# Hybrid attention layer: the probabilities-times-values matmuls of the two head groups made ready together and issued as a pair

## The chip, the cores and the metric

The kernel runs on one core of one Trainium2 chip. The metric is device microseconds from the first to the last instruction of one execution; times of the kernel are medians of several runs. One execution was also taken by the hardware profiler, and all rows below are from it.

## What is computed

One decoder layer for 512 tokens of width 1024 in float32: a norm, an input projection, two attention parts side by side, one output projection, a second norm and a squared-ReLU MLP. The attention is what matters here. Both parts have eight heads of 64 columns. The first part ("NSA") has two groups of four heads with keys and values of their own, and three branches, each with a softmax: over compressed blocks, over selected blocks and over a window. The second part ("DSA") has one set of keys and values for its eight heads, and keeps the 256 best keys of each query. The core of every branch is the same:

```python
s = jnp.einsum('bqhd,bqkd->bhqk', qb, kg) * scale
p = masked_softmax(s, mask)
return jnp.einsum('bhqk,bqkd->bqhd', p.astype(vg.dtype), vg)
```

The change touches the last line alone, the product of probabilities with values.

## The kernel before, in words

**Work units.** Attention runs in 12 units, one for each branch (s: selected, w: window, d: DSA) and each tile of 128 queries (j = 0 to 3); `UNITS` (line 51) gives their order. A unit has two halves. `heads_steps` (line 855) makes, for each of eight heads, scores with two matmuls (lines 872 and 873) into a PSUM bank of tag S, one VectorE pass that adds the mask and finds the maximum (875), and one exponential on ScalarE (876), which leaves the probabilities in SBUF with queries on the partitions. `out_steps` (line 879) first scales the probabilities (`scale`, lines 885 to 893; three heads of four on VectorE, one on GpSimd), then goes over the key blocks kb = 0 to j of 128 keys. For each block and each group g of four heads, `tr` (line 895) transposes four 128 x 128 pieces on TensorE (898) into a PSUM bank of tag T, of which there are two, and copies the bank to an SBUF tile `pt` of 128 x 512 (ScalarE, line 903; VectorE, line 901, for group 1 where j is 3). `pv` (line 906) then multiplies: for each group one matmul (908) with 64 columns of values as weights and the 128 x 512 tile `pt` as the moving operand. Group 0 writes partitions 0 to 63 of the PSUM bank `O`, group 1 partitions 64 to 127. The compressed branch (`cmp_steps`, line 918) does the same with 31 keys, once for each tile of queries: transposes at 953, copies at 955, two matmuls at 960. In all there are 3 x (1 + 2 + 3 + 4) + 4 = 34 such pairs of matmuls, 68 matmuls.

**Dependences.** Each matmul of line 908 or 960 needs the copy of its own group. The matmul of group 0 does not wait for the copy of group 1.

**Order of the work.** The program traces, slot by slot, the heads of one unit interleaved with the output half of the unit before (lines 1071 to 1096), and with other groups of steps, which the table `PLAN` (line 41) puts at slots: sums of the modulation vectors (`vec_steps`, line 703, matmuls at 717; their column sums at 756), the output projection (`outp_steps`, line 998, matmuls at 1008), the loads and splits of its weights (117), the residual and the second norm (1032 to 1058). In program order the transposes of block kb + 1 come before `pv(kb)`. The order in which each engine finally gets its instructions is not this one: the framework's scheduler makes it (line 1198, `schedule_with_timeline_sim=True`), from what is ready in a timeline of its own. Each engine then runs its instructions in that fixed order and waits by semaphores.

**Around it.** The projections come before (up to about 190 us of the span), the MLP after (`up`, line 1115, and `down`, line 1156, from about 397 us to the end).

A float32 matmul stands in the trace as two matmul records with a weight load each; the rows of lines 908 and 960 therefore count two for each matmul.

Of the kernel before, what the change touches and what calls it, by code (L numbers as in the profile page):

```python
# [17 lines left out]
P = 128  # L18
# [19 lines left out]

# Groups of steps in program order: the slot where each begins, and the slots it spreads over.
# Slots 0 to 18 are the projections' pipeline, slots from 19 on the units of attention.  # L40
PLAN = dict(
# [13 lines left out]
def mix(*lists):  # L55
    """One list of the steps of several, each list spread evenly."""
    items = []
    for li, steps in enumerate(lists):
        for i, f in enumerate(steps):
            items.append(((i + 0.5) / len(steps), li, i, f))  # L60
    return [it[3] for it in sorted(items, key=lambda z: z[:3])]
# [8 lines left out]
def layer_kernel(  # L70
# [41 lines left out]
    def bank(tag, name, dt=F32):  # L112
        return psp.tile([P, 512], dt, tag=tag, name=name, bufs=4 if tag == "S" else 2)

    def split(hi, lo, src, eng=V):
        A.copy(hi, src)  # L116
        eng.tensor_tensor(lo, src, hi.bitcast(F32), op=OP.subtract)  # L117
# [3 lines left out]

    # ------------------------------------------------------------ first loads
    wa = w_ada[0].rearrange("(p k) n -> p k n", k=KT)
# [43 lines left out]

    # ------------------------------------------------------------ constants
    ident = cst.tile([P, P], F32, name="ident")
# [23 lines left out]
    def rstd_of(dst, ss):  # L193
        """1 / sqrt(D) of the reciprocal root mean square, from the sums of squares of two halves."""
        m = st([P, 1], "ms")
        G.tensor_scalar(m, ss[:, 0:1], ss[:, 1:2], D * EPS, op0=OP.add, op1=OP.add)  # L196
        G.tensor_tensor(dst, m, mhalf, op=OP.pow)

    # ------------------------------------------------ columns, rope tables
    colT = cst.tile([P, P], F32, name="colT")  # L200
# [40 lines left out]

    # -------------------------------------------------------------- x norms
    rstd = cst.tile([P, NT], F32, name="rstd")
# [17 lines left out]

    # ------------------------- first norm's shift and scale, chunks A and B
    hh = ht("hh", "hh_1")
# [5 lines left out]
    def mod_acc(k):  # L269
        """Sums over the eight slices of c * w_ada, the two halves on different engines."""  # L270
        acc = m2(f"macc_{k}").rearrange("p (u v n) -> p u v n", u=2, v=2)
        macc[k] = acc
        sl = [mod_w[k][i // 4][:, :, i % 4, :] for i in range(KT)]
        steps = []
        for i in range(4):
            dst = acc[:, 1] if i == 0 else sl[i]
            steps.append(lambda i=i, dst=dst: A.activation(dst, sl[i], AF.Copy, scale=c_sb[:, i:i + 1]))
            if i > 0:
                steps.append(lambda i=i: G.tensor_tensor(acc[:, 1], acc[:, 1], sl[i], op=OP.add))
        steps.append(lambda: V.tensor_scalar(acc[:, 0], sl[4], c_sb[:, 4:5], None, op0=OP.mult))  # L280
        for i in range(5, KT):
            steps.append(lambda i=i: V.scalar_tensor_tensor(acc[:, 0], sl[i], c_sb[:, i:i + 1], acc[:, 0],  # L282
                                                            op0=OP.mult, op1=OP.add))
        steps.append(lambda: V.tensor_tensor(acc[:, 0], acc[:, 0], acc[:, 1], op=OP.add))
        return steps
# [95 lines left out]

    # ----------------------------------------------------- projection stages
    def w_unit(view, nm, n=512, eng=V):
# [13 lines left out]
    def rope(src, t, nh, nm, eng):  # L397
        """src: [P, nh, 64] view, rotated in place."""
        t1 = m2("ra_" + nm)[:, :nh * 64].rearrange("p (h d) -> p h d", d=64)
# [143 lines left out]

    # --------------------------------------------------------------- indexer
    work = [None] + [cst.tile([P, (t + 1) * P], F32, name=f"wk_{t}") for t in range(1, NT)]
# [28 lines left out]

    # -------------------------------------------------------------- compress
    kcx = cst.tile([P, 2, 2, 32], F32R, name="kcx")
# [76 lines left out]

    # ------------------------------------------------- G vectors and columns
    res = {}
# [47 lines left out]
    def vec_steps(c0, nm, finish):  # L703
        """finish(half, ps) gets 32 times the sums over 32 partitions each, which add up to c @ w_ada."""
        stt = {}
# [55 lines left out]

    # ------------------------------------------------ the projection pipeline
    def w_in_chunk(c0, c1, nm, eng=V):
# [80 lines left out]

    # ------------------------------------------------------------- attention
    On, Od, o_hl = {}, {}, {}

    class Unit:
        """Eight heads of one branch for one tile of queries."""

# [28 lines left out]
        def out_steps(self, O, first, last):  # L879
# [15 lines left out]
            def tr(kb, g):  # L895
                tp = bank("T", f"tp_{nm}{j}{kb}{g}")
                for i in range(4):
                    PE.transpose(tp[:, i * P:(i + 1) * P], self.P[g * 4 + i][:, kb * P:(kb + 1) * P], ident)  # L898
                pt = m2(f"pt_{nm}{j}{kb}{g}")
                if g == 1 and j >= 3:  # L900
                    V.tensor_copy(pt, tp)
                else:
                    A.copy(pt, tp)
                pts[kb, g] = pt

            def pv(kb):
                for g in range(2):
                    PE.matmul(O[j][g * 64:(g + 1) * 64, :], vn[kb][:, self.vsl[g]:self.vsl[g] + 64], pts[kb, g],  # L908
                              start=(first and kb == 0), stop=(last and kb == j))
            steps += [lambda: scale(0), lambda: scale(1)]  # L910
# [7 lines left out]
    def cmp_steps(j):  # L918
# [31 lines left out]
        def tr(g):  # L950
            tp = bank("T", f"tpc_{j}{g}")
            for i in range(4):
                PE.transpose(tp[0:32, i * P:(i + 1) * P], stt["p"][:, g * 4 + i, :], ident)
            pt = m2(f"ptc_{j}{g}")
            A.copy(pt[0:32, :], tp[0:32, :])
            stt[g] = pt

        def pv():
            for g in range(2):
                PE.matmul(On[j][g * 64:(g + 1) * 64, :], vc[0:31, g, :], stt[g][0:31, :], start=False, stop=True)  # L960
        return [scores, soft1, soft2], [lambda: tr(0), lambda: tr(1), pv]
# [16 lines left out]

    # ---------------------------------------------------- output projection
    wov = w_out[0].rearrange("(b g i d) n -> b g d i n", b=2, g=2, d=64)  # L980
# [81 lines left out]

    # --------------------------------------------- attention, woven together
    wa1, wb1 = wout_steps("a", 1), wout_steps("b", 1)
# [30 lines left out]

    # ------------------------------------------------------------------ MLP
    wuv = w_up[0].rearrange("(k p) n -> p k n", p=P)
# [104 lines left out]
```

## Time and profile before

| what | us |
|---|---|
| median of 3 runs | 760.26 |
| lowest and highest run | 757.55, 763.36 |
| span of the profiled execution | 759.8 |
| TensorE busy in it | 717.0 |
| VectorE busy | 482.5 |
| ScalarE busy | 343.0 |
| GpSimd busy | 160.4 |

The profiled execution has one time on its page, its span from the first to the last instruction; nothing beside it is counted. It is 0.4 us under the median of the runs. Busy times are sums over the whole span; a share of them says nothing of a single stage, so the rows below are taken by stretch.

### The profile page before, as it was taken

Reading aid. Unit: us, or ns where it says so; the run is one execution under the profiler, and the core shown is the slowest. Engines: PE = TensorE matmul, PEld = TensorE weight load, DVE = VectorE, ACT = ScalarE, POOL = GpSimd, SP = SyncE. Lnnn points to the kernel's source line nnn. Section 1 sums busy time; section 2 is a strip of 40 time slices with the busy share of each in tenths; the row PEclk is TensorE's granted clock in tenths of the full one; section 3 lists DMA queues with packets and bytes.
Section 4 is the critical chain, followed back from the end, with each engine's and each line's share of the span. In section 5 each row is a group of like instructions: output and inputs, shape, how many; then the busy total and the mean of one; then the engine's idle time right before and its main releaser. Section 6 shows DMA issues by size and latency. Waiting matters only on the chain.

```text
span 759.8 us, 9830 instructions
## 1 busy us (share of the span) xinstructions
PE 717.0 (94%) x3473; PEld 545.5 (72%) x3473; DVE 482.5 (64%) x1014; ACT 343.0 (45%) x715; POOL 160.4 (21%) x223
## 2 busy tenths in 40 slices
PE   3878989899999999999999999999999999999995
PEld 2667976687755565545579888888888888788884
DVE  5996636979998777772566547463645535344547
ACT  6643683624786568663255532323133223313312
POOL 4663093553632143310202000000000000000003
PEclk9897998878999999999899999999999999999998
DMA  8975452430005380460331336231524332241202
GB/s 277 345 240 160 139 157 66 122 101 1 2 20 153 108 219 1 112 220 2 112 100 40 110 111 194 91 131 60 190 83 141 109 111 82 61 163 56 83 1 110
DMA packets 67610, 87.13 MB, mean 115 GB/s; under 512 B 3973, under 2 KB 38889, under 8 KB 67562
## 3 DMA queue, kind: packets, MB, share of 16 engines
q1 hardware_dynamic: 67562, 86.52, 36.6%
q8 instruction: 27, 0.44, 0.2%
q14 instruction: 21, 0.17, 0.1%
HBM read 84.40 MB, written 2.10 MB: 114 GB/s over the span
## 4 chain that ended last, share of the span: by engine, by line
PE 78%; DVE 10%; DMA 5%; ACT 2%; issue 2%; SPq 2%; POOL 1%; POOLq 0%; DVEq 0%; ACTq 0%
PE up L1115 22%; PE dn L1156 21%; PE O L908 6%; PE op L1008 6%; PE pj_C L316 3%; DMA wv_g<-in_w_ada_dram 2%; PE pj_D L316 2%; PE pA L316 1%; PE tp_d L898 1%; PE tp_w L898 1%; PE tp_s L898 1%; DMA x<-in_x_dram 1%; DVE macc L282 1%; DVE wk L569 1%; DVE m L566 1%
## 5 line engine op out<-in xcount | busy, mean ns | idle before, releaser
L1115 PE MATMUL up<-hh,uh_U 128*128 128x512 f32 (+1 forms) x288 | 104.6, 366 | 0.7 <-ACT hh L116 0.7
L1115 PE MATMUL up<-hh,ul_U 128*128 128x512 f32 (+1 forms) x288 | 105.0, 366 | 0.0
L1115 PE MATMUL up<-hl,uh_U 128*128 128x512 f32 (+1 forms) x288 | 103.9, 366 | 0.4 <-DVE hl L117 0.4
L1156 PE MATMUL dn<-uh_D,al 128*128 128x512 f32 x256 | 99.6, 389 | 0.0
L1156 PE MATMUL dn<-uh_D,ah 128*128 128x512 f32 x256 | 98.7, 391 | 0.0
L1156 PE MATMUL dn<-ul_D,ah 128*128 128x512 f32 x256 | 98.5, 389 | 0.0
L196 POOL TENSOR_SCALAR ms<-sy 128x1 f32<-128x1 f32 x4 | 3.6, 908 | 341.7 <-ACT fj L1135 341.7
L117 DVE TENSOR_TENSOR ul_D<-rw_D,uh_D 128x1024 fp32r<-128x1024 f32 (+1 forms) x35 | 41.3, 1181 | 47.5 <-ACT uh_D L116 45.4
L1162 DVE TENSOR_TENSOR y<-dn,y 128x512 f32<-128x512 f32 x56 | 38.2, 689 | 49.1 <-PE dn L1156 49.1
L1115 PEld LDWEIGHTS up<-hh,uh_U 128*128 128x128 f32 x288 | 54.3, 189 | 9.7 <-ACT hh L116 0.9
L1119 ACT ACTIVATE rl<-up 128x512 f32<-128x512 f32 x32 | 19.1, 596 | 92.7 <-PE dn L1156 59.2
L1115 PEld LDWEIGHTS up<-hh,ul_U 128*128 128x128 f32 x288 | 54.3, 189 | 8.7
L1115 PEld LDWEIGHTS up<-hl,uh_U 128*128 128x128 f32 x288 | 53.7, 189 | 9.4 <-DVE hl L117 0.6
L116 ACT CAST uh_U<-rw_U 128x1024 fp32r<-128x1024 f32 x32 | 33.7, 1052 | 57.3 <-PE dn L1156 51.9
L116 ACT CAST uh_D<-rw_D 128x1024 fp32r<-128x1024 f32 (+1 forms) x36 | 36.3, 1010 | 49.5 <-PE up L1115 37.5
L1156 PEld LDWEIGHTS dn<-uh_D,ah 128*128 128x128 f32 x256 | 48.0, 188 | 10.2 <-issue 0.2
L1156 PEld LDWEIGHTS dn<-uh_D,al 128*128 128x128 f32 x256 | 48.0, 188 | 10.1 <-issue 0.2
L1156 PEld LDWEIGHTS dn<-ul_D,ah 128*128 128x128 f32 x256 | 48.1, 188 | 10.0
L117 DVE TENSOR_TENSOR ul_U<-rw_U,uh_U 128x1024 fp32r<-128x1024 f32 x32 | 39.1, 1221 | 12.9 <-ACT uh_U L116 12.0
L1120 DVE TENSOR_TENSOR rl<-rl 128x512 f32<-128x512 f32 x32 | 22.1, 690 | 34.8 <-ACT rl L1119 34.8
L116 ACT CAST ah<-rl 128x512 fp32r<-128x512 f32 x32 | 19.9, 621 | 29.3 <-DVE rl L1120 29.3
L117 DVE TENSOR_TENSOR al<-rl,ah 128x512 fp32r<-128x512 f32 x32 | 22.0, 688 | 11.0 <-ACT ah L116 11.0
(409 smaller groups left out, 1591.8 us busy)
## 6 DMA issues: line engine op xcount, KB each, us to landing
rw_U<-in_w_up_dram SPq DMA_DIRECT2D x32, 512.0 KB, 4.5
rw_D<-in_w_down_dram SPq DMA_DIRECT2D x32, 512.0 KB, 3.7
wm<-in_w_ada_dram SPq DMA_DIRECT2D x32, 256.0 KB, 5.1
wv_g<-in_w_ada_dram SPq DMA_DIRECT2D x8, 512.0 KB, 6.9
rwo_a<-in_w_out_dram SPq DMA_DIRECT2D x16, 256.0 KB, 5.1
wv_a<-in_w_ada_dram SPq DMA_DIRECT2D x8, 512.0 KB, 4.0
rwo_b<-in_w_out_dram SPq DMA_DIRECT2D x16, 256.0 KB, 4.2
wv_sh<-in_w_ada_dram SPq DMA_DIRECT2D x8, 512.0 KB, 3.6
```

What stands on the lines that cost most here:

```text
L116: A.copy(hi, src)
L117: eng.tensor_tensor(lo, src, hi.bitcast(F32), op=OP.subtract)
L282: steps.append(lambda i=i: V.scalar_tensor_tensor(acc[:, 0], sl[i], c_sb[:, i:i + 1], acc[:, 0], op0=OP.mult, op1=OP.add))
L316: PE.matmul(ps[:, :n], l[:, t, k, :], r[:, k % 2, :n], start=(k == 0 and i == 0), stop=(k == KT - 1 and i == 2))
L898: PE.transpose(tp[:, i * P:(i + 1) * P], self.P[g * 4 + i][:, kb * P:(kb + 1) * P], ident)
L908: PE.matmul(O[j][g * 64:(g + 1) * 64, :], vn[kb][:, self.vsl[g]:self.vsl[g] + 64], pts[kb, g], start=(first and kb == 0), stop=(last and k ...
L1008: PE.matmul(stt["ps"], l[:, kk, :], r[:, kk % 2, :], start=(kk == 0 and i == 0), stop=(kk == 7 and i == 2))
L1115: PE.matmul(pv[:, t0:t1, :], l[:, k % 2, fs], r[:, t0:t1, k, :], start=(n == 0), stop=(n == 23))
L1119: A.activation(rl, ps, AF.Relu)
L1120: V.tensor_tensor(rl, rl, rl, op=OP.mult)
L1156: PE.matmul(ps, l[:, t * P:(t + 1) * P], r[:, f % 2, :], start=(n == 0), stop=(n == 11))
L1162: V.tensor_tensor(ya, ps, ya, op=OP.add)
```

## The change

A helper makes one instruction wait for others. `tr` keeps the copy instruction beside the tile, and `pv` makes the matmul of group 0 wait for the copy of group 1 also. So both matmuls of a pair become ready at the same moment. The same is done in the compressed branch. Nothing else of the code that runs differs; some comments and doc strings are gone.

```diff
+    def after(ins, *others):
+        for o in others:
+            tc.add_manual_dep(ins.ins, o.ins.name,
+                              mybir.DependencyInfo(mybir.DependencyClass.Sync, mybir.DependencyReason.DATA),
+                              reason="pair")
...
                 pt = m2(f"pt_{nm}{j}{kb}{g}")
-                if g == 1 and j >= 3:
-                    V.tensor_copy(pt, tp)
-                else:
-                    A.copy(pt, tp)
-                pts[kb, g] = pt
+                cp = V.tensor_copy(pt, tp) if g == 1 and j >= 3 else A.copy(pt, tp)
+                pts[kb, g] = (pt, cp)
 
             def pv(kb):
-                for g in range(2):
-                    PE.matmul(O[j][g * 64:(g + 1) * 64, :], vn[kb][:, self.vsl[g]:self.vsl[g] + 64], pts[kb, g],
-                              start=(first and kb == 0), stop=(last and kb == j))
+                mm = [PE.matmul(O[j][g * 64:(g + 1) * 64, :], vn[kb][:, self.vsl[g]:self.vsl[g] + 64], pts[kb, g][0],
+                                start=(first and kb == 0), stop=(last and kb == j)) for g in range(2)]
+                after(mm[0], pts[kb, 1][1])
...
             pt = m2(f"ptc_{j}{g}")
-            A.copy(pt[0:32, :], tp[0:32, :])
-            stt[g] = pt
+            stt[g] = (pt, A.copy(pt[0:32, :], tp[0:32, :]))
 
         def pv():
-            for g in range(2):
-                PE.matmul(On[j][g * 64:(g + 1) * 64, :], vc[0:31, g, :], stt[g][0:31, :], start=False, stop=True)
+            mm = [PE.matmul(On[j][g * 64:(g + 1) * 64, :], vc[0:31, g, :], stt[g][0][0:31, :], start=False, stop=True)
+                  for g in range(2)]
+            after(mm[0], stt[1][1])
```

## Rows read from the trace of the kernel before

**Rows 1.** The page: its heading, the engines' busy times (first part) and the chain of work that ended last, by engine (fourth part).

```profile
span 759.8 us, 9830 instructions
...
PE 717.0 (94%) x3473; PEld 545.5 (72%) x3473; DVE 482.5 (64%) x1014; ACT 343.0 (45%) x715; POOL 160.4 (21%) x223
...
PE 78%; DVE 10%; DMA 5%; ACT 2%; issue 2%; SPq 2%; POOL 1%; POOLq 0%; DVEq 0%; ACTq 0%
```

**Rows 2.** The chain of waits over 228 to 397 us of the span alone, its shares by line.

```profile
by line: PE op L1008 26.6%; PE O L908 24.9%; PE tp_d L898 5.2%; PE tp_w L898 5.2%; PE tp_s L898 3.8%; PE O L960 3.5%; PE vs_sh L717 3.3%; DMA rwo_b<-in_w_out_dram 2.7%; PE s_d L872 2.6%; PE vs_a L717 2.5%; PE s_d L873 2.0%; PE s_s L872 2.0%
```

**Rows 3.** The stretches of attention: from and to, length, busy us (and instructions) of PE, PEld, DVE, ACT and POOL, then the granted TensorE clock, the share of DMA and GB/s.

```profile
200.00:230.00 30.00, 28.06 (x160) 18.03 (x159) 28.33 (x123) 26.41 (x87) 12.13 (x18) 1.00 0.08 19
230.00:250.00 20.00, 20.00 (x108) 9.56 (x107) 17.24 (x50) 12.07 (x28) 7.22 (x6) 1.00 0.60 184
250.00:310.00 60.00, 60.00 (x299) 37.27 (x298) 45.66 (x119) 40.28 (x90) 18.35 (x16) 1.00 0.36 97
310.00:350.00 40.00, 39.86 (x192) 20.66 (x189) 26.29 (x60) 20.06 (x46) 6.77 (x8) 1.00 0.46 145
350.00:370.00 20.00, 20.00 (x80) 9.10 (x79) 8.07 (x13) 7.46 (x17) 4.42 (x4) 0.83 0.19 61
370.00:390.00 20.00, 20.00 (x107) 11.77 (x106) 10.32 (x17) 6.96 (x12) 0.86 (x2) 1.00 0.21 68
```

**Rows 4.** Groups of instructions by line, of the whole span, TensorE: line, operation, tiles and shape, count | busy us, mean ns of one | idle before.

```profile
L908 PE MATMUL O<-pt_w,vn 128*64 128x512 f32 x40 | 20.4, 618 | 0.0
L908 PE MATMUL O<-pt_d,vn 128*64 128x512 f32 x40 | 19.3, 618 | 0.0
L908 PE MATMUL O<-pt_s,vn 128*64 128x512 f32 x40 | 18.2, 618 | 0.0
...
L960 PE MATMUL O<-ptc,vc 31*64 31x512 f32 x16 | 8.5, 613 | 0.0
```

**Rows 5.** The timeline of TensorE, lines 908 and 960 alone, where merged rows follow one another: the first and the last of the rows that read x2 (56 of them, between 198.19 and 385.23), and the first and the last of those that read x4 (6 of them, between 271.47 and 381.12). Columns: start, length, engine, line, tiles, shape, count of records.

```profile
198.19 1.07 PE L908 MATMUL O<-pt_s,vn 128*64 128x512 f32 x2
...
385.23 1.07 PE L908 MATMUL O<-pt_d,vn 128*64 128x512 f32 x2
...
271.47 1.08 PE L908 MATMUL O<-pt_s,vn 128*64 128x512 f32 x4
...
381.12 1.08 PE L908 MATMUL O<-pt_d,vn 128*64 128x512 f32 x4
```

**Rows 6.** The timeline of TensorE from 351.77 to 354.92 us, whole.

```profile
351.77 1.07 PE L908 MATMUL O<-pt_w,vn 128*64 128x512 f32 x2
352.78 0.66 PE L898 MATMUL tp_w<-ident,hh_w 128*128 128x128 f32 x4
353.36 1.08 PE L908 MATMUL O<-pt_w,vn 128*64 128x512 f32 x4
354.37 0.61 PE L953 MATMUL tpc<-ident,pc 128*32 128x128 f32 x4
```

**Rows 7.** The timeline of all engines in the last unit, 373 to 383 us, rows of TensorE (PE) and one copy.

```profile
373.18 1.07 PE L717 MATMUL vs_sh<-wv_sh,c_sb 128*32 128x256 f32 x16
...
374.18 0.66 PE L898 MATMUL tp_d<-ident,hl_d 128*128 128x128 f32 x4
...
377.35 0.66 PE L898 MATMUL tp_d<-ident,hl_d 128*128 128x128 f32 x4
...
377.94 1.07 PE L908 MATMUL O<-pt_d,vn 128*64 128x512 f32 x2
378.05 0.69 DVE L901 COPY pt_d<-tp_d 128x512 f32<-128x512 f32 x1 [1.16 <-PE tp_d L898]
...
378.94 0.66 PE L898 MATMUL tp_d<-ident,hl_d 128*128 128x128 f32 x4
...
382.13 0.66 PE L1050 MATMUL hp<-ident,xn 128*128 128x128 f32 x4
...
382.62 0.95 PE L756 MATMUL cv_sh<-ones,acc_sh 128*128 128x1 f32 x8
```

**Rows 8.** Groups of instructions by line, 195 to 395 us, ScalarE and VectorE: the exponential of the widest unit and the copies of transposed probabilities (columns as in group 4).

```profile
L903 ACT COPY pt_d<-tp_d 128x512 f32<-128x512 f32 x16 | 9.2, 585 | 13.0 <-PE tp_d L898 12.7 <-ACT oh L116 0.3
...
L876 ACT ACTIVATE hl_d<-hl_d,mx 128x512 f32<-128x512 f32 x8 | 5.7, 718 | 3.3 <-DVE mx L875 3.2
...
L901 DVE COPY pt_d<-tp_d 128x512 f32<-128x512 f32 x4 | 2.8, 692 | 8.9 <-PE tp_d L898 8.8
```

**Rows 9.** The instructions of line 898 (transposes): the separate waits that TensorE's weight queue carries there, count and ns.

```profile
L898 PEldq EVENT_SEMAPHORE  x8: 51/51/51, 193.0 to 365.5; - x8
```

**Rows 10.** The timeline of TensorE, matmuls of the output projection in two stretches.

```profile
364.01 0.63 PE L1008 MATMUL op<-uoh_b,oh 128*128 128x512 f32 x1
364.44 0.63 PE L1008 MATMUL op<-uoh_b,ol 128*128 128x512 f32 x1
...
368.51 0.40 PE L1008 MATMUL op<-uol_b,oh 128*128 128x512 f32 x1
368.74 0.40 PE L1008 MATMUL op<-uoh_b,oh 128*128 128x512 f32 x1
```

**Rows 11.** Who TensorE's weight loads waited for, 195 to 390 us: us in total, times, longest.

```profile
PEld s_d L872 <- DVE mx L875: 2.5, 3, 0.9
...
PEld tp_d L898 <- ACT pt_d L903: 1.6, 2, 0.8
```

## The prediction

> **What bounds the kernel now.** I read the page first: TensorE is busy 717.0 of 759.8 us, and the chain of work that ended last lies 78% on it [rows 1]. A sum over the span says nothing of the stage that the change touches, so I went on to the chain of waits for 228 to 397 us, which is attention after its first stretch. The reader is to see that nearly all its large entries are TensorE lines, and that the matmuls of lines 908 and 960 hold 24.9% + 3.5% = 28.4% of it [rows 2], that is 0.284 x 169 = 48 us of chain. The busy times by stretch say the same from the other side: from 230 to 390 us TensorE is busy in 159.9 of 160 us, while VectorE, the next busiest, has 107.6 [rows 3]. Before 230 it is otherwise: from 200 to 230 VectorE is busy 28.33 of 30 us, TensorE 28.06 [rows 3]. The waits agree: the longest sum for one form of score matmul on VectorE is 2.5 us, and the transposes of line 898 waited 1.6 us for copies [rows 11]. So from 230 us to the MLP the time goes where TensorE goes, and the MLP after it isn't touched.
>
> **What a pair costs, alone and together.** The 40 + 40 + 40 + 16 = 136 records of lines 908 and 960 [rows 4] are 68 matmuls of two records. In the timeline of TensorE they come as 56 rows of two records, one matmul with something else on either side, and as 6 rows of four, both matmuls of a pair next to each other [rows 5]. This is the view on which everything rests, because the kernel before does by chance, six times, what the change wants always. A row of two begins at 351.77 and the next instruction at 352.78: 1.01 us. A row of four begins at 353.36 and the next at 354.37: 1.01 us as well [rows 6]. The second matmul costs nothing: the two use different halves of the array's columns and run at the same time. The sum of modulation vectors shows the same at a quarter of the columns: sixteen records, eight matmuls, are through in 374.18 - 373.18 = 1.00 us [rows 7].
>
> The Trainium skill, in "TensorE: Matmul & The Clock Gate", Part 3, under what overlaps and what doesn't, has a rule against this: a weight load overlaps a matmul in flight only if the two use different groups of rows. Both matmuls of a pair use all 128 rows and differ in columns alone, so by that rule the second would follow the first and the change would bring next to nothing. The rows of four at 1.01 us speak against it.
>
> **What is removed.** 56 rows of two become 28 rows of four. For each pair one row of 1.01 us goes. With it goes one change into this form: four transposes ahead of such a matmul take 377.94 - 377.35 = 0.59 us, four ahead of a full-width matmul 382.62 - 382.13 = 0.49 us [rows 7], so 0.10 us more. I take 1.1 us for a pair; 28 pairs are 31 us of TensorE time, which is the end above which nothing can come.
>
> **What of it lies on the path.** Of the 56 rows, 10 start before 230 us and 46 after, and by stretch the 46 are 8, 14, 13, 6 and 5 [counted as in rows 5, stretches as in rows 3]. Half of each times 1.1 us gives 4.4, 7.7, 7.2, 3.3 and 2.8 us. What VectorE has idle in the same stretches bounds it: 20 - 17.24 = 2.8, 60 - 45.66 = 14.3, 40 - 26.29 = 13.7, 11.9 and 9.7 us. Only the first is cut, to 2.8. The sum after 230 us is 2.8 + 7.7 + 7.2 + 3.3 + 2.8 = 23.8 us. Before 230 us five pairs would give 5.5, but VectorE has 30 - 28.33 = 1.7 us idle there; I take 1.7. Together 25.5 us.
>
> **What is added: a wait.** The matmul of group 0 now waits for the copy of group 1. No row before shows this wait, so I bound it. Transposes that begin at 377.35 have their copy begin at 378.05 and last 0.69 us [rows 7], so it is done 1.39 us after they began, while TensorE is through with them after 0.59. If nothing stands between, TensorE waits 0.80 us. Upper end: 0.80 for each of 28 pairs, 22.4 us. Lower end: zero, where one other 1 us piece stands between. That the wait saves time by itself I exclude, as it only holds something back. The nearest case is the last unit, where one set of transposes (0.59 us) stands between a set and its matmul [rows 7]: 0.80 - 0.59 = 0.2 us, which I take. 28 x 0.2 = 5.6 us. Where a copy is on ScalarE it lasts 0.585 us instead of 0.692 [rows 8], inside this. Behind the waiting matmul in TensorE's queue are the next unit's scores, the next block's transposes and the output projection, so the maximum on VectorE and the exponentials wait with it; they have the idle time named above.
>
> For the 12 pairs with j = 3 the two copies are on two engines, and the matmul may need a wait instruction of its own: 0.051 us in TensorE's weight queue [rows 9], 12 x 0.05 = 0.6 us, or nothing if it is carried by the matmul. I take 0.6. The first group's `pt` tile is held until the pair has run, up to 1 us longer; it has six buffers, and the copies on ScalarE sat idle 13.0 us waiting for transposes in one form alone [rows 8], so I put it at nothing; without that cover a copy would come later by the same up to 1 us, which the upper end of the wait stands for.
>
> No other instruction, byte or DMA is added or moved to another engine. Loads of the output projection's weights and of the MLP are asked for earlier as their buffers come free earlier; DMA is at 0.46 of its time at most after 250 us [rows 3], so they find room.
>
> **Sum.** 25.5 - 5.6 - 0.6 = 19.3 us less. The profiled execution had 759.8, so 740.5 us; the median of the runs stands 0.4 above it, so I forecast 741 us. VectorE is late next: in the stretch from 230 to 250 us it would be busy all the time.
>
> **The clock.** In 350 to 370 us the granted clock averages 0.83 [rows 3], with output-projection matmuls 0.43 us apart against 0.23 later [rows 10]: the lower level, 1.2 GHz, for (1 - 0.83) x 20 / 0.5 = 6.8 us, after a stretch of single 64-column matmuls and transposes [rows 6]. It costs up to 3.4 us. A changed order can lose this stretch or get a second one: 3.4 us either way, in the range and not in the sum.
>
> **Rivals.**
> 1. The pairs don't stay together. Ready at once doesn't mean issued at once: the framework's scheduler may put a score matmul or a projection matmul, earlier in the program, between the two. For: before, 28 pairs of 34 stood apart. Against: they stood apart because each became ready with its own copy, and the next block's transposes, which do come first in the program, are ready no later than the first matmul. If half of the 28 are split, half of the 25.5 is left: 12.7 - 6.2 = 6.5 us, 753 us.
> 2. VectorE and ScalarE become the bound through their chain of scores, maximum, exponential, scaling and transposes, and TensorE then waits for them in an order that was made for slower pairs. For: VectorE's 94% in 200 to 230 us. Against: its 67% after it. If half of the 19.3 is lost so, 750 us.
> 3. Slower. Copies stand in ScalarE's queue behind exponentials of the next unit, 0.72 us each [rows 8], and TensorE now stands still for the second copy at every pair. The gain is gone where the mean wait is over (25.5 - 0.6) / 28 = 0.9 us: one exponential ahead of each second copy (0.2 + 0.72 = 0.92 us). With two (1.64 us) it is 28 x 1.64 - 24.9 = 21 us slower, 781 us. For: such copies and exponentials share the engine in every unit. Against: transposes waited only 1.6 us for copies [rows 11], and the second copy is on VectorE where j is 3.
> 4. The two matmuls of a pair run one after the other, as the skill's rule would have it. Then only the 0.10 us of the change of form is saved, 2.8 us, less the 6.2 of waits: 763 us. Against it are the six rows of four.
>
> **How the numbers follow.** The forecast has 0.72 with a range of its own from 733 to 749; rival 1 has 0.09, rival 2 0.13, rival 3 0.04, rival 4 0.02. What a measurement of this kernel can tell from no change is about 1%, 7.6 us: faster is under 752.7. Forecast and rival 2 lie there, with a third of rival 1 and none of the rest, less a little for rival 2's far end: 0.72 + 0.11 + 0.03 = 0.86. Slower over 1% is most of rival 3: 0.03. The remaining 0.11 is the same. The range runs from 732 (near all of the 25.5 with the slow clock gone, 759.8 - 25.5 - 3.4 = 731) to 752, to hold most of rival 2 and leave out two in ten.
>
> **What would show it.** Right: some 34 rows of four on lines 908 and 960, each with the next instruction 1.01 us later; attention from 230 us to the first MLP matmul shorter by about 18 us; the MLP unchanged. The waits: weight loads of line 908 with VectorE or ScalarE copies as releaser, about 6 us in all. Wrong: many rows of two left (rival 1); VectorE over 85% busy after 230 us and TensorE with idle time for the maximum of line 875 (rival 2); more than 25 us of waits at line 908 (rival 3); rows of four of 2 us (rival 4).

## The result, and the profile after

The changed kernel takes 738.9 us (median of 4 runs, 736.85 to 741.29), the kernel before 760.2 beside it (757.55 to 763.36). The ratio is 0.971, 95% interval 0.968 to 0.975: 21.3 us less, where 741 had been forecast. The profiled execution is the fastest of the four runs; its span is 735.1 us against 759.8 [rows 1], so 24.7 us are to be found in the two traces. They are more than the 21.3 us of the medians, because the executions were not alike: the time of a run stands 1.7 us (changed kernel) or about 2 us (kernel before) above its span, so the profile before belongs to an execution some 1.5 us slower than its median and the other to one 2 us faster. In the changed kernel's program the transposes are line 905, their copies 907, the pair's matmuls 911 (compressed branch: 957, 959, 962), the scores 879 and 880, the maximum 882, the exponential 883.

The page of the changed kernel: heading, busy times, chain by engine.

```profile
span 735.1 us, 9839 instructions
...
PE 686.9 (93%) x3473; PEld 541.7 (74%) x3473; DVE 485.3 (66%) x1014; ACT 341.8 (46%) x715; POOL 160.5 (22%) x223
...
PE 75%; DVE 14%; DMA 3%; issue 3%; ACT 2%; POOL 1%; SPq 0%; POOLq 0%; DVEq 0%; ACTq 0%
```

TensorE has the same 3473 instructions as before and is busy 30.1 us less. Its idle time rose from 42.8 to 48.2 us, so 5.4 of the 30.1 us came back as waiting. The two make up the difference of the spans: 30.1 - 5.4 = 24.7. Not all of the 30.1 us is the pairs: the granted clock averages 0.963 of full speed in the one execution and 0.966 in the other, so that 0.037 x 759.8 = 28.1 us were lost to it before and 0.034 x 735.1 = 25.0 us after, 3.1 us less.

Nothing changed in the MLP. Its first matmul starts 363.2 us before the end in both; the first fence is the kernel before, the second the changed one.

```profile
396.58 0.27 PE L1115 MATMUL up<-hh,uh_U 128*128 128x256 f32 x1
```

```profile
371.90 0.28 PE L1119 MATMUL up<-hh,uh_U 128*128 128x256 f32 x1
```

All 34 pairs now stand as rows of four; [rows 5] had 6 of them. The timeline of TensorE in the changed kernel: three such rows, each with the instruction after it.

```profile
219.13 1.77 PE L911 MATMUL O<-pt_s,vn 128*64 128x512 f32 x4
220.83 0.39 PE L879 MATMUL s_d<-k1a,qE 128*128 128x256 f32 x1
...
339.41 1.07 PE L962 MATMUL O<-ptc,vc 31*64 31x512 f32 x4 [0.23 <-ACT ptc L959]
340.41 1.05 PE L763 MATMUL cv_sh<-ones,acc_sh 128*128 128x1 f32 x8
...
351.54 1.08 PE L911 MATMUL O<-pt_d,vn 128*64 128x512 f32 x4
352.55 0.66 PE L905 MATMUL tp_d<-ident,hl_d 128*128 128x128 f32 x4
```

From a row's start to the next instruction it is 1.00 and 1.01 us in the last two. The row at 219.13 takes 1.70: most of it lies where the granted clock is at its lower level, 1.2 GHz (0.50 of full speed from 213.74 to 220.56 us). Summed over all of them, start to next start, lines 908 and 960 held 62.2 us of TensorE before (62 rows), and lines 911 and 962 hold 36.6 us now (34 rows).

In the chain of waits over 228 to 372 us (one row, as the view gives it) line 911 has 13.8% of 144 us, 20 us, where [rows 2] had 24.9% of 169 us, 42 us.

```profile
by line: PE op L1012 29.9%; PE O L911 13.8%; PE tp_w L905 4.7%; PE tp_s L905 4.2%; PE tp_d L905 3.5%; DMA rwo_b<-in_w_out_dram 3.4%; issue 3.1%; DVE P_d L900 2.6%; DMA wv_sh<-in_w_ada_dram 2.4%; PE s_d L879 2.3%; PE vs_sh L724 2.1%; PE s_d 
```

The stretches of attention in the changed kernel, columns as in [rows 3]:

```profile
200.00:230.00 30.00, 28.21 (x160) 20.65 (x159) 29.82 (x128) 26.77 (x87) 10.52 (x16) 0.83 0.07 18
230.00:250.00 20.00, 18.35 (x120) 10.00 (x118) 20.00 (x47) 14.31 (x34) 7.30 (x6) 1.00 0.70 211
250.00:310.00 60.00, 56.74 (x321) 39.32 (x320) 49.91 (x124) 40.75 (x94) 21.98 (x19) 0.99 0.42 114
310.00:350.00 40.00, 39.62 (x235) 23.47 (x237) 26.97 (x60) 21.56 (x52) 8.20 (x8) 0.97 0.46 158
350.00:372.00 22.00, 21.42 (x122) 14.48 (x122) 14.74 (x24) 12.40 (x24) 1.34 (x4) 1.00 0.19 58
```

Three things stand in it beside the shorter total. VectorE is full from 230 to 250 us, with TensorE idle for 1.65 us there. TensorE lost 3.26 us in 250 to 310. And the granted clock of 200 to 230 us fell from 1.00 to 0.83, while the 0.83 of 350 to 370 in [rows 3] is gone.

The loss in 250 to 310 us is one stall. ScalarE in the changed kernel, then TensorE (in brackets: idle time before the instruction, and what ended it):

```profile
307.09 1.04 ACT L123 CAST uoh_b<-rwo_b 128x1024 fp32r<-128x1024 f32 x1 [5.83 <-DMA rwo_b<-in_w_out_dram]
308.04 0.72 ACT L883 ACTIVATE hh_w<-hh_w,mx 128x512 f32<-128x512 f32 x1
...
308.76 0.56 ACT L907 COPY pt_s<-tp_s 128x512 f32<-128x512 f32 x1
```

```profile
305.73 0.39 PE L880 MATMUL s_w<-k2w,qC 128*128 128x512 f32 x1
309.37 1.97 PE L905 MATMUL tp_s<-ident,hl_s 128*128 128x128 f32 x8 [3.26 <-ACT pt_s L907]
```

ScalarE's next instruction is the cast of an output-projection weight that hasn't landed. It waits 5.83 us, and an exponential and a copy of transposed probabilities, whose inputs are ready by 304.3 us, wait behind it. TensorE runs out of work and stands until that copy has emptied its PSUM bank. Right behind the stall its granted clock is at the lower level for 3.4 us, 309.3 to 312.7. The chain of waits of the changed kernel over 295 to 310 us tells how the load came to be late:

```profile
301.54 0.57 POOL ro L204
302.11 0.01 SPq L994
...
302.16 4.85 DMA rwo_b<-in_w_out_dram
...
307.09 0.10 ACT uoh_b L123
...
308.04 0.81 ACT hh_w L883 x2
308.85 0.48 ACT pt_s L907
...
309.37 0.69 PE tp_s L905 x2
```

The transfer itself took 4.85 us. The DMA engines were all but idle before it (a share of 0.06 from 300 to 302 us) and full while it ran (1.04 from 302 to 307 us, where a load for the MLP goes beside it); the median load of these weights lands after 4.0 us. So about 1 us of the wait can be the full DMA. The rest is a late request: SP's queue, which asks for the loads in a fixed order, waits for the readers of earlier loads (over 190 to 372 us: us in total, times, longest):

```profile
SPq L994 <- POOL uol_b L124: 18.9, 2, 15.4
...
SPq L994 <- DVE uol_b L124: 7.1, 1, 7.1
```

Little of these waits is the readers' own work. The GpSimd subtraction that ends the wait of 15.4 us lasts 2.39 us (289.31, shown with e11 below), and before it came ScalarE's cast at 288.20. In the kernel before ScalarE's longest wait for such a load is 2.2 us, at 319 us, and TensorE is busy 39.86 of the 40 us there [rows 3].

### The profile page after: what moved, and what is told of

It is laid out like the page before. It is cut to its first block, busy times and chain, and to the rows that moved or that the text cites. A ratio compares the mean times of both kernels' runs of the same rounds, so it can differ in the third digit from the quotient of the medians.

```text
span 735.1 us, 9839 instructions
## 1 busy us (share of the span) xinstructions
PE 686.9 (93%) x3473; PEld 541.7 (74%) x3473; DVE 485.3 (66%) x1014; ACT 341.8 (46%) x715; POOL 160.5 (22%) x223
## 4 chain that ended last, share of the span: by engine, by line
PE 75%; DVE 14%; DMA 3%; issue 3%; ACT 2%; POOL 1%; SPq 0%; POOLq 0%; DVEq 0%; ACTq 0%
PE up L1119 23%; PE dn L1160 22%; PE op L1012 6%; PE O L911 3%; PE pj_E L323 2%; DVE macc L289 2%; PE pA L323 2%; PE pj_D L323 2%; PE pj_C L323 2%; PE tp_s L905 1%; DMA x<-in_x_dram 1%; PE pB L323 1%; PE tp_w L905 1%; PE hid_v L628 1%; DMA wv_g<-in_w_ada_dram 1%
## 5 line engine op out<-in xcount | busy, mean ns | idle before, releaser
L1160 PEld LDWEIGHTS dn<-uh_D,al 128*128 128x128 f32 x256 | 48.1, 188 | 10.2 <-issue 0.2
L1160 PEld LDWEIGHTS dn<-uh_D,ah 128*128 128x128 f32 x256 | 48.0, 188 | 10.2 <-issue 0.2
```

The costliest lines, as they stand in the source:

```text
L1160: PE.matmul(ps, l[:, t * P:(t + 1) * P], r[:, f % 2, :], start=(n == 0), stop=(n == 11))
```

## The experiments

The kernel before was timed beside each group of them: 759.68 us with e1 to e4, 761.14 with e5 to e8, 760.17 with e9 to e11 and 761.28 with e12. A ratio is to that time. All but e5, e9 and e12 are edits of the changed kernel; where one is set against 738.9 us, the two were timed at different times.

### e1: pairs kept together, but 19 of the 34 in one half of the columns

```diff
-                 mm = [PE.matmul(O[j][g * 64:(g + 1) * 64, :], vn[kb]...
+                 one = nm == "w" or (nm == "s" and kb > 0) or (nm == "d" and 0 < kb < j)
+                 mm = [PE.matmul(O[j][0 if one else g * 64:64 if one else (g + 1) * 64, :], vn[kb]...
```

> The changed kernel, but in 19 of the 34 pairs both matmuls write partitions 0 to 63 of the bank, so that they stand next to each other and can't use different halves of the array's columns; the upper half of the bank lacks these products. 15 of the 19 lie after about 250 us. Theory (the gain is the overlap of the two halves): rows of four of about 2 us in place of 1.01, and 15 x 0.9 to 19 x 1.0, that is 13 to 19 us, over the changed kernel's 738.9: 752 to 758 us. Rival (the gain is from the order that the added dependence brings): 737 to 742 us.

Measured 756.4 us, ratio 0.996 (0.994 to 0.997). The timeline of TensorE in it, a pair in two halves and a pair in one half, each with the instruction after it:

```profile
307.10 1.08 PE L911 MATMUL O<-pt_d,vn 128*64 128x512 f32 x4
308.11 0.50 PE L1012 MATMUL op<-uoh_a,ol 128*128 128x512 f32 x1
...
311.03 1.93 PE L911 MATMUL O<-pt_d,vn 128*64 128x512 f32 x4
312.89 0.66 PE L905 MATMUL tp_s<-ident,hl_s 128*128 128x128 f32 x4
```

1.01 us against 1.86. All 34 pairs are adjacent and have the same added wait; 19 x 0.85 = 16.2 us account for nearly all of the 17.5 us by which this kernel is slower than the changed one. In its profile TensorE is busy 15.6 us more (702.5), and idle 4.7 us more; the planner gave this kernel an order of its own. The gain is the concurrency of the two column halves. (A pair in one half also adds into the same partitions of PSUM; this run doesn't separate the two.) The stall of the changed kernel stands in this one as well, though 19 of its pairs take 1.86 us:

```profile
321.27 1.12 PE L905 MATMUL tp_s<-ident,hl_s 128*128 128x128 f32 x4 [4.27 <-ACT pt_s L907]
```

### e4: the same wait, but one set of transposes between the two matmuls of 18 pairs

```diff
+            def tr1(kb):
+                m0 = one(kb - 1, 0); after(m0, pts[kb - 1, 1][1])
+                with tc.issue_after(m0.ins): t = tr(kb, 1)
+                with tc.issue_after(t.ins): one(kb - 1, 1)
...
-                steps += [lambda kb=kb: tr(kb, 0), lambda kb=kb: tr(kb, 1)]
-                if kb > 0:
-                    steps.append(lambda kb=kb: pv(kb - 1))
+                steps += [lambda kb=kb: tr(kb, 0), lambda kb=kb: tr1(kb) if kb else tr(0, 1)]
```

> The changed kernel with its added wait, but in the 18 pairs that have a next block of keys the next block's transposes of group 1 are put between the two matmuls; 16 pairs stay together. 15 of the 18 lie after about 250 us. Theory: each split pair costs 1.0 to 1.1 us more where TensorE is the bound: 753 to 759 us. Rival (order and wait bring the gain, not the neighbourhood): within 3 us of 738.9.

Measured 753.8 us, ratio 0.992 (0.989 to 0.995). Its timeline of TensorE, one split pair whole:

```profile
304.75 1.07 PE L910 MATMUL O<-pt_d,vn 128*64 128x512 f32 x2
305.75 0.66 PE L904 MATMUL tp_d<-ident,hh_d 128*128 128x128 f32 x4
306.33 1.07 PE L910 MATMUL O<-pt_d,vn 128*64 128x512 f32 x2
307.34 0.50 PE L879 MATMUL s_w<-k1w,qC 128*128 128x512 f32 x1
```

By the added wait both matmuls are ready at 304.75, and yet four transposes between them make each cost its own 1.01 us. 14.9 us lost over 18 pairs is 0.83 for each. Ready together isn't enough: they must be neighbours in TensorE's queue.

### e2 and e3: the wait for j < 2 alone, and for j of 2 and 3 alone

```diff
-                after(mm[0], pts[kb, 1][1])
+                if j < 2: after(mm[0], pts[kb, 1][1])
```

(e3 has `j >= 2`; both do the same in the compressed branch.)

> The added dependence for the tiles of queries 0 and 1 alone (10 pairs, up to about 250 us). If VectorE is the bound in this stretch, as the prediction's sum has it: 1 to 5 us less than the kernel before, 755 to 759 us. If every pair is worth 1.1 us wherever it stands: 11 us less, 749 us.

> The added dependence for the tiles of queries 2 and 3 alone (24 pairs, of which 6 stood together before; 18 new). Theory: 18 x 1.1 = 20 us less, less up to 5 us of waits: 740 to 745 us, so that this part alone brings nearly the whole gain. Rival (gain spread evenly over pairs, 21.3 us x 18 / 28 = 13.7): 746 to 748 us.

The numbers of pairs in these expectations are one off: tiles 0 and 1 have 3 x (1 + 2) + 2 = 11 pairs, tiles 2 and 3 have 23, of which 17 are new. The traces agree: 62 rows before, 51 in e2, 45 in e3.

e2 took 754.8 us, ratio 0.993 (0.990 to 0.995): 4.9 us for 11 pairs, 0.45 each, and by the interval at most 0.7. e3 took 745.9 us, ratio 0.981 (0.977 to 0.985): 13.8 us for 17 pairs, 0.81 each, by the interval 0.69 to 1.03. An early pair is worth less than its 1.01 us, as forecast; that a late one is worth less too isn't clear of the noise. If it is, one reason stands in e3's timeline of TensorE, the same stall as in the changed kernel:

```profile
319.82 1.97 PE L905 MATMUL tp_s<-ident,hl_s 128*128 128x128 f32 x8 [3.30 <-ACT pt_s L907]
```

With 3.3 us put back it would be 17.1 us, 1.01 for each late pair. The profiled run took 750.0 us, 4.2 more than the median, so it isn't shown that the median holds the whole stall.

### e5, e6, e9, e10: less and more VectorE work under both kernels

The forecast took 5.4 us off the sum (3.8 before 230 us, 1.6 after) because VectorE has no idle time there. To test that, the search for the best keys of the last tile of queries was left out (some 23 us of VectorE's instructions; its busy time fell by 15.1 us in the kernel before and 18.2 in the changed one), or made 24 rounds instead of 16, which keeps 192 keys instead of 128 for that tile and leaves all shapes after it alone. (With 512 tokens the second part keeps 128 keys; the 256 named at the head of this document is the bound for longer inputs.)

```diff
-        return [lambda: topk_round(t)] * 16 + [
+        return [lambda: topk_round(t)] * (16 if t < 3 else 0) + [
```

(e5 before and e6 changed; e9 and e10 have `else 24`.)

> The kernel before without the 16 rounds of the top-k for the last tile of queries (maximum and replace on VectorE, 23 us of its time between about 200 and 270 us; the mask of that tile is left without its selection). In the kernel before, VectorE is the bound only up to about 230 us: if that is so, most of the 23 us lies beside TensorE's work and 3 to 8 us are saved: 752 to 757 us. If VectorE bounds all of attention: 20 us or more, under 740 us.

> The same 16 rounds left out of the changed kernel. Theory: with paired matmuls VectorE is the bound from 190 to 260 us (busy 9.9 of 10 us there in the profile after), so the cut brings more here than in the kernel before, 8 to 13 us: 726 to 731 us. Rival (TensorE is still the bound, the pairs bring the same wherever VectorE stands): the same saving as in the kernel before, 731 to 736 us.

> The kernel before, with 24 instead of 16 rounds in the search for the largest scores of the last tile of queries: the last 8 rounds find nothing that the output needs, so this adds about 8 x (0.684 + 0.675 + 0.08) = 11.5 us of VectorE work in the stretch 190 to 260 us and changes nothing else by intent. Theory (VectorE is the bound of that stretch once the pairs stand together, and not quite before): the kernel before loses a part of it, 763 to 768 us beside 760. Rival (VectorE has as much cover in both kernels, and the planner lays other work over the addition): 758 to 762 us. Read together with the same edit in the changed kernel.

> The changed kernel with the same 8 added rounds, 11.5 us of VectorE work in 190 to 260 us. Theory (VectorE bounds that stretch in the changed kernel): it loses most of the addition, 8 to 11.5 us, so 747 to 751 us beside 738.9, and more than the same edit costs the kernel before. Rival (TensorE bounds it still, and the busy VectorE has work that can wait): under 3 us, 737 to 742 us. A loss equal to that of the kernel before says that VectorE was as much a bound before as after, so that it took nothing from the gain.

| VectorE work of the last tile's search | kernel before | changed | quotient of the ratios |
|---|---|---|---|
| left out | 767.9 (1.009) | 744.0 (0.978) | 0.970 |
| as it is | 760.2 (1) | 738.9 (0.971) | 0.971 |
| half as much again | 767.7 (1.011) | 745.5 (0.981) | 0.970 |

Both directions made both kernels slower, by 5 to 8 us. Three of the four expectations missed; e9's time was in the theory's range, but e10 lost no more than e9 (6.6 us against 7.6), which contradicts the theory. What doesn't move is the gain: the change is worth 3% whichever the load on VectorE. The stretch 190 to 260 us, one row for each kernel: the changed one, e6, e10.

```profile
190.00:260.00 70.00, 66.03 (x404) 45.66 (x403) 69.58 (x233) 53.19 (x149) 25.98 (x35) 0.93 0.30 91
```

```profile
190.00:260.00 70.00, 63.86 (x392) 44.26 (x392) 50.55 (x191) 51.74 (x150) 27.05 (x36) 0.92 0.28 78
```

```profile
190.00:260.00 70.00, 65.24 (x379) 44.16 (x377) 66.59 (x232) 50.42 (x150) 26.68 (x36) 0.87 0.27 76
```

VectorE is busy 69.58 of 70 us in the changed kernel and 50.55 in e6. If a full VectorE were what holds TensorE there, TensorE's idle time would shrink with it. It grew from 3.97 to 6.14 us. And e10, with more VectorE work in the program, shows less of it in this stretch: the planner put it elsewhere. Each of the four kernels has an order of its own, so the tests carry a disturbance as large as the effect looked for. That VectorE cost a part of the 5.4 us can't be excluded: the quotients are known to about 0.4 to 0.7% each, 3 to 5 us. That VectorE was the bound is not shown, and the rows of e6 speak against it. What makes an early pair worth 0.45 us, and why leaving work out costs time, stays open.

### e7, e8 and e11: three ways at the stall of 301 to 307 us

```diff
- wb1a=(28, 0.122)
+ wb1a=(29.05, 0.122)
```

> The changed kernel with one group of output-projection weight loads and splits (wb1a) put at slot 29.05 in place of 28. In the profile after, ScalarE stands 5.8 us at 301 to 307 us before the cast of such a weight tile, whose DMA has not landed, with exponentials and copies queued behind it, and TensorE is idle for 3.3 us. If this stall is an accident of the order in ScalarE's queue: 3 us less, 734 to 737 us. Rival (the loads are late anyway and the stall only moves): 738 to 742 us.

Measured 737.7 us, ratio 0.971 (0.967 to 0.974): no gain that can be told. The stall moved, it didn't go. ScalarE and TensorE of e7:

```profile
307.95 1.05 ACT L123 CAST uoh_b<-rwo_b 128x1024 fp32r<-128x1024 f32 x1 [3.20 <-DMA rwo_b<-in_w_out_dram]
```

```profile
311.73 0.66 PE L905 MATMUL tp_s<-ident,hl_s 128*128 128x128 f32 x4 [2.22 <-ACT pt_s L907]
```

In e8 GpSimd scales two heads of four for j of 1 and 2, to unload VectorE:

```diff
-                    if h % 4 >= 3:
+                    if h % 4 >= (2 if j in (1, 2) else 3):
```

> The changed kernel with two heads of four scaled on GpSimd in place of one, for the tiles of queries 1 and 2 (12 instructions of 0.39 to 0.46 us leave VectorE, 5 us in all, most before 270 us). If VectorE bounds that stretch now: 1 to 4 us less, 735 to 738 us. Rival (GpSimd takes 0.6 to 0.9 us for one and the transposes wait for it): 739 to 744 us.

Measured 740.7 us, ratio 0.974 (0.972 to 0.977): nothing gained, as its rival said.

In e11 the subtraction that ends the split of a `b` weight goes from GpSimd to VectorE. In the changed kernel GpSimd needs 2.39 and 2.55 us for one (VectorE 1.2), and SP's queue waits for it:

```profile
289.31 2.39 POOL L124 TENSOR_TENSOR uol_b<-rwo_b,uoh_b 128x1024 fp32r<-128x1024 f32 x1 [2.08 <-ACT uoh_b L123]
...
296.18 2.55 POOL L124 TENSOR_TENSOR uol_b<-rwo_b,uoh_b 128x1024 fp32r<-128x1024 f32 x1
```

```diff
-            split(hi, lo, rw, G if ip == 0 else V)
+            split(hi, lo, rw, G if ip == 0 and key == "a" else V)
```

> The changed kernel, with the halves of the b keys' weights that GpSimd takes apart given to VectorE, so that the buffers of the raw weights come free earlier and the load of rwo_b, for which ScalarE waited 5.8 us at 301 to 307 us, starts earlier. Theory (the stall of 3.3 us that TensorE showed before tp_s at 309 us is part of the time): 735 to 737.5 us. Rival (the stall is slack, or VectorE's added work costs as much elsewhere): 738 to 742 us.

Measured 734.7 us (733.03 to 735.40), ratio 0.966 (0.963 to 0.970): 4.2 us under the changed kernel, and its slowest run is under the fastest of that one, though the intervals of the two ratios overlap a little. ScalarE's wait for the load fell from 5.83 to 1.18 us, and TensorE is idle 0.39 us of 300 to 320 where it was idle 3.41. ScalarE of e11, then its stretches 300 to 320 us:

```profile
304.85 0.72 ACT L883 ACTIVATE hh_w<-hh_w,mx 128x512 f32<-128x512 f32 x1 [0.40 <-DVE mx L882]
...
305.58 0.56 ACT L907 COPY pt_s<-tp_s 128x512 f32<-128x512 f32 x1
307.32 1.05 ACT L123 CAST uoh_b<-rwo_b 128x1024 fp32r<-128x1024 f32 x1 [1.18 <-DMA rwo_b<-in_w_out_dram]
```

```profile
300.00:310.00 10.00, 10.00 (x57) 5.96 (x56) 9.14 (x18) 6.63 (x15) 1.53 (x4) 1.00 0.57 158
310.00:320.00 10.00, 9.61 (x73) 4.60 (x74) 10.00 (x28) 7.05 (x17) 2.84 (x3) 1.00 0.80 254
```

The same two stretches of the changed kernel, where the granted clock is lower too, (0.03 + 0.14) x 10 = 1.7 us of full speed:

```profile
300.00:310.00 10.00, 6.74 (x34) 3.77 (x32) 6.49 (x15) 4.17 (x11) 2.24 (x3) 0.97 0.60 157
310.00:320.00 10.00, 9.85 (x65) 4.97 (x63) 8.48 (x21) 7.55 (x19) 1.79 (x2) 0.86 0.61 209
```

It is the fastest of all. The request itself is not earlier by the clock: SP's last one for these weights ends at 303.54 us, in the changed kernel at 302.76. But the last pair of the unit d, j = 2, starts at 305.62 us here and at 302.61 there, so relative to TensorE's work the load is asked for 2.2 us earlier. And the order differs: the exponential and the copy that stood behind the cast now stand ahead of it. Which of the two took the stall away isn't separated. The work that VectorE takes over starts at 270 us, so it isn't added to the stretch of 230 to 250 us where VectorE was full.

### e12: the same edit in the kernel before

The line of e11, in the kernel before.

> The kernel before, with the same halves of the b keys' weights given to VectorE instead of GpSimd as in e11. Theory (the wait for rwo_b that this shortens is one that the change brought: the kernel before has no such stall, so nothing to win): 758.5 to 762 us beside 760. Rival (the earlier loads, or a GpSimd with less to do, help either kernel, so that e11's 4 us say nothing of the stall): 754 to 757.5 us.

Measured 759.5 us beside 761.28, ratio 1.000 (0.998 to 1.003): nothing. So e11's gain isn't a better split as such. It takes away what came in with the change, and without it the change is worth 0.966/1.000, some 26 us. Whether the shorter work of TensorE or the new order brought the stall is open: e1, where TensorE's work is 15.6 us longer, has it too.

## Why the prediction was right

**The pair, the main step, held.** 1.1 us of TensorE for each of 28 pairs made 31; TensorE's busy time fell by 30.1. By starts, lines 908 and 960 gave back 62.2 - 36.6 = 25.6; four of the 34 rows run partly at the lower clock (206.40, 213.28, 219.13 and 311.27) and take 2.1 us more than 1.01, so 28 pairs would have given 27.7, 0.99 for each. The 0.10 us for the change of form isn't confirmed: of the 30.1 us the rows leave 4.5, and that much can be the clock alone, which took 3.1 us less than before in all and 2.1 more in the rows, so 5.2 less outside them. Four of the six rows of four before are, by their order, not a pair but the second matmul of one and the first of the next (the one at 316.51 among them); they too use both halves, so the price of 1.01 us stands, and so does the count of 28 rows less. Rival 4 is out by e1: two matmuls in one half take 1.86 us, in two halves 1.01. Rival 1 is out by the 34 rows of four. The weight loads of a pair don't wait for its first matmul to end: all four of the row at 351.54 are through in 0.20 us, while its first matmul runs.

```profile
351.53 0.20 PEld L911 LDWEIGHTS O<-pt_d,vn 128*64 128x64 f32 x4 [0.17 <-issue]
```

The rule of the Trainium skill, "TensorE: Matmul & The Clock Gate", Part 3, that a weight load overlaps a matmul in flight only where their groups of rows differ, isn't borne out by this row. The Trainium skill has another statement in the same part, under its measured speedups: 2.38 times for three matmuls packed by columns. Here two give 1.86 / 1.01 = 1.84 times, so the traces agree with it in kind.

**The wait was priced too high.** 5.6 us for waits and 0.6 for wait instructions were taken off. The idle time before lines 911 and 962 in the changed kernel, in us and times:

```profile
  issue: 5.2, 23
  ACT pt_s L907: 1.0, 3
...
  ACT ptc L959: 0.7, 2
```

Waits for these copies are 1.7 us in all, five of them, and neither line has a wait instruction of its own in TensorE's queues. The 1.7 us counts the weight queue too; the matmuls themselves were idle for 0.4 us, twice 0.2. The step that failed is the 0.2 us for each pair, read off the last unit, where one set of transposes stands between a set and its matmul. That case came once, and as priced: the row at 339.41 starts 1.27 us after the transposes of its second group began and waits 0.23 us (the other wait is at the first row of all, 196.32). At the 33 others more stands between (scores, projection matmuls, further transposes or the pair before), at least 2.08 us from those transposes' start, where the forecast had the copy done after 1.39. The lower end, zero, was nearer. Rival 3 priced the mean wait that cancels the gain at 0.9 us; it was at most 1.7 / 28 = 0.06.

**The late stretches were taken at full price.** After 250 us the forecast credits each pair with 1.1 us and only the wait against it. e3 gave 0.81, and the stall before `tp_s` is a cost that no step had: 3.3 us of TensorE, some 4 us by e11 and e12. It isn't a wait of the pair. It is what the forecast passed over when it wrote that loads asked for earlier find room because DMA is at most 0.46 busy [rows 3]. The mean over a stretch didn't show what mattered. The queue that asks for the loads was late, waiting for readers on GpSimd and VectorE; the DMA, idle before, was then full while the load ran; and ScalarE's queue stood behind the load.

**These two errors cancelled.** 6.2 us taken off for waits against at most 1.7 measured is 4.5 too many; the stall is about 4 too few. With both set right the sum would be 759.8 - 25.5 + 1.7 + 4 = 740.0, 0.4 us more as a median, so 741 was right with more luck than its working shows. Its sign for the stretch missed: from 230 us to the MLP's first matmul it is 141.9 us against 166.6, 24.7 less, where about 18 were forecast.

**VectorE as the cap in the first stretch.** That it would be busy all the time from 230 to 250 us came out to the digit, 20.00 of 20. The amount agrees too: the forecast had 1.7 + 2.8 for the early pairs, and e2, which holds nearly these pairs, gave 4.9 (3.6 to 7.7 by its interval). But the reason isn't shown: e6, e9 and e10 left the gain where it was when VectorE's load was changed. The size was right, its cause is open. Rival 2's sign, VectorE over 85% after 230 us with TensorE idle for the maximum, was seen in 230 to 250 alone; over 250 to 310 VectorE has 49.91 of 60, 83%.

**The clock.** Up to 3.4 us either way was in the range. The profiled execution lost the slow stretch of 350 to 370 us and has more time at the lower level earlier: (1 - 0.83) x 30 / 0.5 = 10.2 us in 200 to 230 us, where [rows 3] had none. This may be a part of why early pairs give less. But e9, the kernel before with more search, has 0.83 there as well, so it doesn't take the pairs to bring it.

## What to carry to other kernels

Two matmuls that use different halves of the array's columns cost one if they are neighbours in TensorE's queue, and two if four transposes stand between them; making both wait for the later operand made them neighbours (all 34 pairs here, 33 of 34 in e6), and costs little where TensorE has other work queued ahead. When a change gives the bounding engine less work or a new order, look for loads that other engines' in-order queues wait for: here the next loss was a request that came late, because readers of earlier loads were late, with ready work queued behind it. And a row that shows an engine full doesn't prove that it bounds: take work from it and see whether the other engine's idle time shrinks.

## What was not expected of the hardware

Leaving out some 23 us of VectorE work made both kernels slower, by 6.7 and about 5 us, and TensorE idled more, 6.14 us against 3.97 in 190 to 260: with an order fixed ahead, a lighter load gave another order and not a faster one. And a wait for the later of two copies, at all 34 pairs, cost 1.7 us at most.
